# A rotation by 180 degrees: part of the first load moved to a second DMA queue

## The chip, the cores and the metric

The kernel runs on one core of a Trainium2 chip. The metric is device time in microseconds (us). "Span" is the profile's time from a core's first instruction to its last; it is about 1.8 us shorter than the device time of the same execution.

## The reference

```python
def setup_inputs():
    batch, c, h, w = 32, 3, 256, 256
    return {"x": np.random.randn(batch, c, h, w).astype(np.float32)}

def reference(x):
    return np.rot90(x, k=2, axes=(-2, -1)).astype(np.float32)
```

Each of the 96 planes of 256 x 256 elements, read as one row of 65,536 elements, has to come out reversed. That is 25.17 MB in and 25.17 MB out.

## The kernel before

The planes form three groups of 32. A group is a tile of 128 partitions by 16,384 elements (64 KB per partition), four partitions per plane. VectorE reverses each partition in place, swapping 2,048-element blocks through a scratch tile T; the store reverses the order of the four partitions of a plane.

```python
    A = pool.tile([P, E], x.dtype, tag="A")      # P = 128, E = 16384
    Bt = pool.tile([P, E], x.dtype, tag="B")
    Ct = pool.tile([P, E], x.dtype, tag="C")
    # ... T, back(), copy()
    def load(t, g, lo, hi):
        return nc.sync.dma_start(out=t[:, lo:hi], in_=x4[g][:, lo:hi])

    def store(t, g, lo, hi):
        return nc.sync.dma_start(
            out=o4[g][:, ::-1, lo:hi], in_=t[:, lo:hi])
    # ... inside(t): 12 copies on VectorE
    TAIL = 1536
    load(A, 0, 0, E)
    load(Bt, 1, 0, E)
    body = load(Ct, 2, 0, E - TAIL)
    load(Ct, 2, E - TAIL, E)
    inside(A)
    LEAD = 128
    store(A, 0, 0, LEAD)
    first = store(A, 0, LEAD, E)      # made to wait for `body`
    # ...
    for g, t in ((1, Bt), (2, Ct)):
        inside(t)
        store(t, g, 0, E)
```

All eight DMAs go through SyncE's queue. The big store of A waits until the body of C has landed; a last strip of C (6 KB per row) and a small store (512 B per row) are meant to keep the DMA engines busy while that store is issued.

Of the kernel before, what the change touches and what calls it, by code (L numbers as in the profile page):

```python
# [2 lines left out]

os.environ.setdefault("NEURON_RT_ULTRASERVER_MODE", "4")

# [4 lines left out]


@with_exitstack
def kernel(
    ctx: ExitStack,
    tc: tile.TileContext,
    x: bass.AP,
    out: bass.AP,
):








    nc = tc.nc
    P = 128

    B, C, H, W = x.shape
    L = H * W
    G = 32
    E = L // 4
    J = E // 8

    x4 = x.rearrange("b c h w -> (b c) (h w)").rearrange(
        "(g n) (s e) -> g (n s) e", n=G, s=4)
    o4 = out.rearrange("b c h w -> (b c) (h w)").rearrange(
        "(g n) (s e) -> g n s e", n=G, s=4)  # L40

    pool = ctx.enter_context(tc.tile_pool(name="slots", bufs=1))
    A = pool.tile([P, E], x.dtype, tag="A")
    Bt = pool.tile([P, E], x.dtype, tag="B")
    Ct = pool.tile([P, E], x.dtype, tag="C")
    T = pool.tile([P, J], x.dtype, tag="T")

    def back(t, lo, hi):
        return t[:, hi - 1:(lo - 1 if lo else None):-1]

    def copy(dst, src):
        tc.keep_in_program_order(nc.vector.tensor_copy(out=dst, in_=src))  # L52

    def load(t, g, lo, hi):
        return nc.sync.dma_start(out=t[:, lo:hi], in_=x4[g][:, lo:hi])  # L55

    def store(t, g, lo, hi):
        return nc.sync.dma_start(
            out=o4[g][:, ::-1, lo:hi], in_=t[:, lo:hi])

    def inside(t):
        for lo in range(0, E // 2, J):
            hi = E - lo - J
            copy(T[:, :], back(t, hi, hi + J))
            copy(t[:, hi:hi + J], back(t, lo, lo + J))
            copy(t[:, lo:lo + J], T[:, :])

    TAIL = 1536
    load(A, 0, 0, E)
    load(Bt, 1, 0, E)  # L70
    body = load(Ct, 2, 0, E - TAIL)
    load(Ct, 2, E - TAIL, E)
# [3 lines that stand above are left out]
    first = store(A, 0, LEAD, E)  # L76
    tc.add_manual_dep(
        first.ins, body.ins.name,
        mybir.DependencyInfo(mybir.DependencyClass.Sync, mybir.DependencyReason.DATA),
        reason="the first store is queued while the last strip is on its way")  # L80
# [5 lines that stand above are left out]
# [1 line left out]
_INS = ['x']  # L87
_OUTS = [((32, 3, 256, 256), 'float32')]


# [23 lines left out]
```

## Time and profile before

| | before |
|---|---|
| device time, median of 3 (lowest to highest) | 122.09 us (121.91 to 122.40) |
| span of the profiled execution | 120.2 us |
| VectorE busy | 44.2 us, 37% |
| DMA engines busy | 97.5% |
| first DMA packet, last completion write | 1.77 us, 119.05 us |

The last row comes from the trace's list of DMA packets: start, duration, size and queue of each. No view prints them, so they are given as numbers in the text. With each DMA, every one of the 16 DMA engines gets eight of the 128 rows, one packet per row, and ends it with a 4-byte completion write. The lines of the page itself are in the prediction.

### The profile page before, as it was taken

Reading aid. Unit: us, or ns where it says so; the run is one execution under the profiler, and the core shown is the slowest. Engines: PE = TensorE matmul, PEld = TensorE weight load, DVE = VectorE, ACT = ScalarE, POOL = GpSimd, SP = SyncE. Lnnn points to the kernel's source line nnn. Section 1 sums busy time; section 2 is a strip of 40 time slices with the busy share of each in tenths; the row PEclk is TensorE's granted clock in tenths of the full one; section 3 lists DMA queues with packets and bytes.
Section 4 is the critical chain, followed back from the end, with each engine's and each line's share of the span. In section 5 each row is a group of like instructions: output and inputs, shape, how many; then the busy total and the mean of one; then the engine's idle time right before and its main releaser. Section 6 shows DMA issues by size and latency. Waiting matters only on the chain.

```text
span 120.2 us, 95 instructions
## 1 busy us (share of the span) xinstructions
DVE 44.2 (37%) x36; POOL 0.2 (0%) x4
## 2 busy tenths in 40 slices
DVE  0000000499995099999059999400000000000000
POOL 0000000000000000000000000000000000000000
DMA  9889988898889879879499777988898889888980
GB/s 349 349 349 393 654 349 349 349 676 371 349 349 633 382 316 593 356 316 633 190 440 692 346 346 346 692 349 349 349 698 349 349 349 698 349 349 349 676 371 0
DMA packets 1152, 50.33 MB, mean 419 GB/s; under 512 B 128, under 2 KB 256, under 8 KB 384
## 3 DMA queue, kind: packets, MB, share of 16 engines
q1 hardware_dynamic: 1152, 50.33, 97.5%
HBM read 25.17 MB, written 25.17 MB: 419 GB/s over the span
## 4 chain that ended last, share of the span: by engine, by line
DMA 34%; DVE 25%; another core or an unknown queue 4%; issue 1%; SPq 0%; DVEq 0%
DMA Bt<-in_x_dram 34%; DVE T L52 8%; DVE Bt L52 8%; DVE Ct L52 8%; SPq L55 0%; DVEq L52 0%
## 5 line engine op out<-in xcount | busy, mean ns | idle before, releaser
L52 DVE COPY T<-A 128x2048 f32<-128x2048 f32 x4 | 4.9, 1227 | 22.7 <-DMA A<-in_x_dram 22.6
L52 DVE COPY T<-Ct 128x2048 f32<-128x2048 f32 x4 | 4.9, 1227 | 4.5 <-DMA Ct<-in_x_dram 4.4
L52 DVE COPY T<-Bt 128x2048 f32<-128x2048 f32 x4 | 4.9, 1227 | 4.4 <-DMA Bt<-in_x_dram 4.3
L52 DVE COPY Bt<-Bt 128x2048 f32<-128x2048 f32 x4 | 4.9, 1227 | 0.1
L52 DVE COPY A<-T 128x2048 f32<-128x2048 f32 x4 | 4.9, 1227 | 0.1
L52 DVE COPY Bt<-T 128x2048 f32<-128x2048 f32 x4 | 4.9, 1227 | 0.1
L52 DVE COPY Ct<-T 128x2048 f32<-128x2048 f32 x4 | 4.9, 1227 | 0.1
L52 DVE COPY Ct<-Ct 128x2048 f32<-128x2048 f32 x4 | 4.9, 1227 | 0.1
L52 DVE COPY A<-A 128x2048 f32<-128x2048 f32 x4 | 4.9, 1227 | 0.1
L98 POOL MEMSET const-bfloat16-1.0<- 128x1 bf16 x1 | 0.1, 102 | 0.0
L98 POOL MEMSET const-uint8-127<- 128x1 uint8 x1 | 0.1, 101 | 0.0
L98 POOL MEMSET const-float32-0.0<- 128x1 f32 x1 | 0.1, 99 | 0.2 <-issue 0.2
L98 POOL MEMSET const-float32-1.0<- 128x1 f32 x1 | 0.1, 98 | 0.0
## 6 DMA issues: line engine op xcount, KB each, us to landing
out_dram<-A SPq DMA_DIRECT2D x1, 8128.0 KB, 21.2
Ct<-in_x_dram SPq DMA_DIRECT2D x1, 7424.0 KB, 57.8
Ct<-in_x_dram SPq DMA_DIRECT2D x1, 768.0 KB, 59.3
out_dram<-A SPq DMA_DIRECT2D x1, 64.0 KB, 35.2
A<-in_x_dram SPq DMA_DIRECT2D x1, 21.9
Bt<-in_x_dram SPq DMA_DIRECT2D x1, 40.7
out_dram<-Bt SPq DMA_DIRECT2D x1, 39.9
out_dram<-Ct SPq DMA_DIRECT2D x1, 42.8
```

The lines of the kernel that those rows point to most:

```text
L52: tc.keep_in_program_order(nc.vector.tensor_copy(out=dst, in_=src))
L98: nc = _bacc.Bacc("TRN2", target_bir_lowering=False, num_devices=1)
```

## The change

The intent is to have two engines start the first load at the same time. ScalarE issues the first 2 KB of each row of A and SyncE the other 62 KB, so that the stream of data might begin sooner or denser.

```diff
-    def load(t, g, lo, hi):
-        return nc.sync.dma_start(out=t[:, lo:hi], in_=x4[g][:, lo:hi])
+    def load(t, g, lo, hi, queue=nc.sync):
+        return queue.dma_start(out=t[:, lo:hi], in_=x4[g][:, lo:hi])
@@
     TAIL = 1536
-    load(A, 0, 0, E)
+    HEAD = 512
+    load(A, 0, 0, HEAD, nc.scalar)
+    load(A, 0, HEAD, E)
     load(Bt, 1, 0, E)
```

## The prediction

> **What bounds the kernel now.** I read the page from the top: busy shares first, then the slices, the queue line, the chain, and last the trace's own list of DMA packets, which no view prints. Engines and data movement are told apart at once.
>
> ```profile
> span 120.2 us, 95 instructions
> DVE 44.2 (37%) x36; POOL 0.2 (0%) x4
> DMA  9889988898889879879499777988898889888980
> DMA packets 1152, 50.33 MB, mean 419 GB/s; under 512 B 128, under 2 KB 256, under 8 KB 384
> q1 hardware_dynamic: 1152, 50.33, 97.5%
> ```
>
> The reader is to see that VectorE works 37% of the span while the sixteen DMA engines are busy for 97.5% of it: 0.975 x 120.2 us = 117.2 us. The whole tensor goes in and out once (25.17 MB each way), so the bytes cannot shrink. There is one queue, q1: everything is issued by SyncE.
>
> The chain of waits in order of time begins like this (start, duration, what):
>
> ```profile
> 0.66 0.07 issue
> 0.73 0.39 SPq L55
> 1.12 0.06 issue
> 1.18 40.74 DMA Bt<-in_x_dram
> ```
>
> It then follows VectorE through groups B and C, which is only how the view walks back over semaphores. That VectorE does not set the end is seen from the last store: it is issued at 76.62 us, when the store of A, queued at 59.53, has not yet landed (59.53 plus 21.2 in the table of issues is 80.7), and B's lies behind that. The last store takes 42.8 us to land only because it queues. Cutting the span into stages shows the same; the columns are the stretch, its length, VectorE busy, GpSimd busy, clock, DMA share and GB/s:
>
> ```profile
> 0.00:1.20 1.20, 0.00 (x0) 0.20 (x4) 1.00 0.00 0
> 1.20:21.90 20.70, 0.00 (x0) 0.00 (x0) 1.00 0.99 415
> 21.90:59.50 37.60, 29.45 (x24) 0.00 (x0) 1.00 0.99 429
> 59.50:76.60 17.10, 14.72 (x12) 0.00 (x0) 1.00 1.06 456
> 76.60:119.40 42.80, 0.00 (x0) 0.00 (x0) 1.00 0.96 416
> 119.40:120.20 0.80, 0.00 (x0) 0.00 (x0) 1.00 0.00 0
> ```
>
> A packet is counted in whole, so shares over 1.00 are an artefact of where I cut. What matters: DMA is full from the first stage to the last, and bare only in the first one to two and the last one microsecond.
>
> From the packet records, counted from the span's start: the first packets start between 1.77 and 2.21 us (mean 1.93), and the last completion write ends at 119.05. The difference is 117.28 us, and each engine is on average busy for 117.17 us of it. So there is **no hole to fill between the first packet and the last**. The budget is 1.77 us of front, 117.28 us of packets, 1.14 us from the last packet to the end.
>
> One slow place stands inside the 117.28. A row of 64 KB is one packet; it takes 2.418 us from the second row on, but about 3.19 us for the first row of each engine, and the second row's packet starts on average 3.13 us after the first's (5.06 against 1.93). So the cold start of the stream costs 3.13 - 2.42 = 0.71 us, once. Only this and the front are anywhere near the changed load.
>
> The front is made of the barrier between engines, one DMA issue, and a latency. The timeline (start, duration, engine, line):
>
> ```profile
> 0.73 0.39 SPq L55 DMA_DIRECT2D A<-in_x_dram  x1
> 1.18 0.42 SPq L55 DMA_DIRECT2D Bt<-in_x_dram  x1
> 1.63 1.01 SPq L55 DMA_DIRECT2D Ct<-in_x_dram  x2
> ```
>
> SyncE starts its first issue at 0.73; the first packet starts 1.04 us later, at 1.77. The next issues are done at 2.64, long before the 20 us of A's packets run out, so issue time after the first never shows.
>
> **What the Trainium skill says.** The page "DMA: Bandwidth & Descriptors", section "Issuing engines are not separate DMA queues", says that DMAs started by different engines run on the same 16 DMA engines and that using several saves only sequencer time. The trace before has only one queue and cannot show it, but it shows how little sequencer time there is to save: one 0.39 us issue lies ahead of the first packet. The same page, section "Queues, rings and completion order", says each DMA engine alternates between the queues that have work, at packet granularity; no run here shows it yet. Section "Where 436 GB/s comes from" gives a ceiling of 435.2 GB/s for 16 ports. The trace agrees closely: 16 x 65,536 B / 2.418 us = 433.6 GB/s. Section "Latency and other measured facts" gives about 0.6 us to the first byte for DMAs from SyncE and ScalarE alike; here 0.65 us pass from the end of the first issue (1.12) to the first packet (1.77).
>
> **The change part by part.**
>
> *Added:* one DMA on ScalarE's queue, 128 rows of 2 KB. The order of instructions shows just that: one copy of 128x512 on ScalarE, SyncE's first copy now 128x15872 in place of 128x16384, everything else unchanged. In the trace before, ScalarE leaves the starting barrier at 0.652 us and SyncE at 0.647 (raw event times), so ScalarE should issue at about 0.74, beside SyncE and not ahead of it. Front saved: 0, because the head's first packet needs the same issue and the same latency.
>
> *Cost of the split:* each row becomes two packets. I fit the packet time from sizes in this trace: 512 B takes 27 ns, 6,144 B takes 234 ns, 65,536 B takes 2,418 ns. The line through the outer two is 8.2 ns + 36.8 ns per KB (6 KB: 229, close to 234). So a 2 KB packet takes about 82 ns, of which 8.2 is new. Eight rows per engine give 8 x 8.2 = 66 ns, plus one more completion write of 9 ns: **+0.07 us** of DMA time. This lies on the bounding path, as the stream has no slack.
>
> *Shape of the big load:* it is no longer contiguous in memory. The strided body of C was issued in 432 ns (raw), A in 387. If the first packet waits for the issue to end, SyncE's part begins 45 ns later, but the head is then already in work. I take +0.02 us.
>
> *Cold start:* 0.71 us are lost on each engine's first packet. If that is latency of the first read, both queues pay it at once and nothing changes. If it is a ramp with too few reads in flight, two queues with one packet each could shorten it. I give this an expected **-0.15 us**, from a fifth of 0.71; this is my choice, not a measurement.
>
> *VectorE:* its first copy waits for the end of A at 22.6 us and would move by about 0.1. It waits again at 42.0 and 61.5 for loads, so the shift is absorbed. C's last copy ends at 76.6, while the store of A lands only at 80.7 and B's at 100, so there is over 20 us of slack. The store's waiting for the body of C at 59.5 shifts along with the stream.
>
> The sum is 0 + 0.07 + 0.02 - 0.15 = -0.06 us on 122.09, rounded to **122.0 us**.
>
> **The rivals.**
>
> *The head fills the front.* If SyncE's 64 KB issue were slow because of its size, 2 KB rows could start flowing sooner. For it: 1.04 us from issue to packet is long. Against it: SyncE's four load issues take 387 to 533 ns, and the shortest rows (6 KB) took the longest, so rows' length is not what an issue costs. It would be worth 0.2 to 0.4 us, so some 121.7 to 121.9.
>
> *The second queue gets in the way.* Both issuing engines make descriptors at the same moment; if that is shared work, each engine's first packets come later. The first packets of one DMA already spread over 0.44 us, so a second could add about as much. Switching between queues after each packet may also break read-ahead: with 16 switches of, say, 20 to 50 ns, 0.3 to 0.8 us would be lost. The trace of one queue does show packets back to back, so it has something to lose. This makes 122.4 to 122.9.
>
> *ScalarE issues late.* Then its packets mix into the stream later, and A lands by the same total of bytes. The time stays at 122.1 to 122.2, as no hole opens.
>
> **Range and chances.** The executions of the kernel before spread from 121.91 to 122.40, so the noise alone is about 0.25 either way. The first rival pulls down by 0.3, the second up by 0.5. I take 121.6 to 122.5. To be 2% faster, 2.4 us would have to go; the whole front and the cold start together are 1.77 + 0.71 = 2.48 us, most of it barrier and latency that the change doesn't touch. To be 2% slower, the head would have to cost 2.4 us, about 30 times its worked-out cost of packets. So: faster 0.01, same 0.98, slower 0.01.
>
> **What would show each step right or wrong.** A second queue should appear with 128 packets and 0.26 MB. The first packet should start within 0.1 us of 1.77; clearly earlier, by 0.2 or more, means the first rival. Busy time of the DMA engines should grow by under 0.1 us each; if it grows by 0.3 or more, switching queues costs. The second row of 62 KB should start later than the first by as much as before, less 2 KB's worth; a shorter distance means that the cold start is a ramp. VectorE's first copy should begin within 0.3 us of 22.6 and the last store be issued near 76.6. The prediction fails if the stream gets a hole of microseconds anywhere, most likely around 20 to 22 us, where A hands over to B, or if ScalarE's queue needs some setting-up that SyncE's doesn't.

## The result, and the profile after

| | before | after |
|---|---|---|
| device time, median of 6 (lowest to highest) | 122.12 us (121.91 to 122.65) | 122.01 us (121.96 to 122.07) |
| ratio, 95% interval | | 0.9983 (0.9963 to 1.0003) |
| first packet, last completion write | 1.77 us, 119.05 us | 1.76 us, 119.06 us |
| DMA busy per engine | 117.17 us | 117.24 us |

A ratio is taken from the runs of both kernels in the same rounds, so it is not quite the ratio of the medians quoted.

The page of the changed kernel, the lines that answer to those of before:

```profile
span 120.2 us, 97 instructions
DVE 44.2 (37%) x36; POOL 0.2 (0%) x4
DMA  9888988899889879979499777988898889888990
DMA packets 1296, 50.33 MB, mean 419 GB/s; under 512 B 144, under 2 KB 272, under 8 KB 528
q1 hardware_dynamic: 1152, 50.07, 97.0%
q10 hardware_dynamic: 144, 0.26, 0.6%
```

A second queue, q10, has appeared with 128 packets of 2 KB and 16 completion writes. The shares add up to 97.6%, where one queue had 97.5%: the same work, spread over two queues. The timeline of the start (start, duration, engine, line):

```profile
0.73 0.38 ACTq L55 DMA_DIRECT2D A<-in_x_dram  x1
0.73 0.39 SPq L55 DMA_DIRECT2D A<-in_x_dram  x1
1.18 0.42 SPq L55 DMA_DIRECT2D Bt<-in_x_dram  x1
...
22.62 1.23 DVE L52 COPY T<-A 128x2048 f32<-128x2048 f32 x1 [22.62 <-DMA A<-in_x_dram]
```

Both issues start at 0.73 us. SyncE issues no earlier and no faster than before, and VectorE gets A at 22.62 us in both kernels. The same stages as before (stretch, length, VectorE, GpSimd, clock, DMA share, GB/s):

```profile
0.00:1.20 1.20, 0.00 (x0) 0.20 (x4) 1.00 0.00 0
1.20:21.90 20.70, 0.00 (x0) 0.00 (x0) 1.00 1.01 423
21.90:59.50 37.60, 29.45 (x24) 0.00 (x0) 1.00 0.98 423
59.50:76.60 17.10, 14.67 (x12) 0.00 (x0) 1.00 1.07 459
76.60:119.40 42.80, 0.05 (x1) 0.00 (x0) 1.00 0.96 416
119.40:120.20 0.80, 0.00 (x0) 0.00 (x0) 1.00 0.00 0
```

No stage got shorter. The first seems denser (1.01 against 0.99) and the second thinner by the same, because whole packets fall to one side of the cut. The issues of A with their KB and the time to landing:

```profile
A<-in_x_dram SPq DMA_DIRECT2D x1, 7936.0 KB, 21.9
...
A<-in_x_dram ACTq DMA_DIRECT2D x1, 256.0 KB, 22.0
```

This pair says most: 256 KB took as long to land as 7,936 KB. The packet list shows why. Each engine begins with a 62 KB packet of SyncE's queue, then takes one 2 KB packet of ScalarE's, then again one of SyncE's, and so on for eight rows. The "head" is not ahead: its first packet starts at 4.78 us, when the first 62 KB packet ends, and its last one ends with A.

In the kernel before, the two lines to compare with, of its issues and of its timeline, are:

```profile
A<-in_x_dram SPq DMA_DIRECT2D x1, 21.9
...
22.62 1.23 DVE L52 COPY T<-A 128x2048 f32<-128x2048 f32 x1 [22.62 <-DMA A<-in_x_dram]
```

### The profile page after: what moved, and what is told of

Same layout as the page of the kernel before. It is cut to its first block, busy times and chain, and to the rows that moved or that the text cites. A ratio compares the mean times of both kernels' runs of the same rounds, so it can differ in the third digit from the quotient of the medians.

```text
span 120.2 us, 97 instructions
## 1 busy us (share of the span) xinstructions
DVE 44.2 (37%) x36; POOL 0.2 (0%) x4
## 4 chain that ended last, share of the span: by engine, by line
DMA 34%; DVE 25%; another core or an unknown queue 4%; issue 1%; SPq 0%; DVEq 0%
DMA Bt<-in_x_dram 34%; DVE T L52 8%; DVE Bt L52 8%; DVE Ct L52 8%; SPq L55 0%; DVEq L52 0%
```

## The experiments

My theory: the DMA stream bounds the kernel from its first packet to its last; front and cold start are the same for one queue and two; the split costs a few nanoseconds per packet. Rival one: the second queue fills the front or shortens the cold start, and the split hides part of the gain. Rival two: turns between queues cost time, and some gain at the start hides that.

### The split alone, on one queue

```diff
-    load(A, 0, 0, HEAD, nc.scalar)
+    load(A, 0, 0, HEAD)
     load(A, 0, HEAD, E)
```

> The same split (2 KB and 62 KB per row), but both loads from SyncE's queue, head first. Theory (the stream bounds, a packet costs 8.2 ns more, front and cold start are common to both queues): 122.1 to 122.2 us, mean DMA busy per engine 117.24 us as in the changed kernel, ratio to the kernel before 0.998 to 1.002. First row of packets: the 2 KB packet absorbs the cold start and takes about 0.7 + 0.08 us. Rival (the second queue fills the front or shortens the cold start): this kernel loses what the second queue gained, so 0.1 to 0.4 us slower than the changed kernel of the same rounds, and the first megabyte lands later.

Measured: 122.12 us (121.96 to 122.64), before 122.17, ratio 0.9994 (0.9973 to 1.0015). Against the kernel before, moving the split back to one queue changes nothing that these rounds resolve, and against the changed kernel of the same rounds (122.10) it loses nothing: the 0.1 to 0.4 us of rival one is not seen. The other sign named for rival one did appear: the first megabyte (10^6 bytes) was in at 5.52 us, against 5.14 to 5.23 in three traces of the changed kernel. That mark is coarse, because packets count when they end, and here eight heads per engine end before any 62 KB packet does. My detail missed: the sixteen 2 KB packets that start first took 0.08 to 0.51 us (mean 0.19), not 0.78. Yet A was landed, on average over the engines, at 21.92 us, as in the three kernels with unsplit rows (21.92 to 21.96). So the cold start isn't a fixed delay charged to whichever packet is first; it is spread over the packets of the first microseconds.

### The changed kernel again, and the kernel before as its own rival

No edit: the changed kernel and the kernel before are each run as an experiment.

> The changed kernel itself in more rounds, beside the kernel before. Theory: the 0.11 us by which its median was lower is noise, the true difference is +0.07 us from the split; ratio 0.998 to 1.002 with 1 inside the interval. Rival (a real gain from the second queue): ratio about 0.998 again, with 1 outside the interval.

> The kernel before, unchanged, submitted as if it were an experiment: shows how far two equal kernels differ in the same rounds. Every theory expects 1.000; the deviation seen is the noise that a difference of 0.1 us has to be held against. I expect up to 0.2%.

Measured: changed kernel 122.10 us, ratio 0.9990 (0.9971 to 1.0009); kernel before against itself 122.11 us, ratio 0.9987 (0.9969 to 1.0004). In these rounds a kernel "beats" its own copy by 0.13%. A single ratio of 0.998 proves nothing here.

### The roles swapped

```diff
-    load(A, 0, 0, HEAD, nc.scalar)
-    load(A, 0, HEAD, E)
+    load(A, 0, 0, HEAD)
+    load(A, 0, HEAD, E, nc.scalar)
```

> The 2 KB heads from SyncE's queue and the 62 KB parts from ScalarE's, while the loads of B and C follow on SyncE's. Theory: the two queues alternate packet by packet, eight packets each, so A still lands at 22 us, and the time is 122.1 to 122.2 us, busy 117.24 us per engine. Which packet comes first tells whether SyncE's queue always goes first (then 2 KB first) or ScalarE's, or the larger. Rival (second queue gets in the way of the first): the queue with B's packets behind it takes turns beyond the heads, A lands late (up to 40 us), and the time may grow by some tenths.

Measured: 122.50 us (121.94 to 122.62), ratio 1.0013 (0.9992 to 1.0034): unresolved, at most a third of a percent slower. My detail missed again. The timeline of this kernel, VectorE's first copy:

```profile
25.66 1.23 DVE L52 COPY T<-A 128x2048 f32<-128x2048 f32 x1 [25.66 <-DMA A<-in_x_dram]
```

A was usable 3 us later than in the changed kernel. In the packet list, the sixteen packets that start first are again of SyncE's queue, as in the changed kernel, so it is the queue and not the size that went first in these two. The engines took 32 heads, two each on average, before their first 62 KB packets, so the heads ran out one row early. The last 62 KB packets of A start at 19.76 us on average, but the completion write that reports them comes at 24.52: one 64 KB packet of B, 2.4 us long, goes between. Five of six runs were 122.34 or slower, so I suspect a real loss of a few tenths. In the profiled execution the engines' completions of A were spread over 1.22 us, against 0.44 in the changed kernel; why this matters is taken up below.

### Many turns between queues, and the same pieces on one queue

```diff
-    load(A, 0, 0, HEAD, nc.scalar)
-    load(A, 0, HEAD, E)
+    CHUNK = 512
+    for odd, queue in ((1, nc.scalar), (0, nc.sync)):   # one queue: nc.sync twice
+        pieces = A[:, :].rearrange("p (k two c) -> p k two c", two=2, c=CHUNK)
+        source = x4[0].rearrange("p (k two c) -> p k two c", two=2, c=CHUNK)
+        queue.dma_start(out=pieces[:, :, odd, :], in_=source[:, :, odd, :])
```

> A is loaded in 2 KB pieces, odd pieces from ScalarE's queue, even ones from SyncE's: 256 packets per engine for A in place of 8. Theory: 248 more packets of 8.2 ns each give +2.03 us, so 124.1 us, busy 119.2 us per engine. Rival (changing between queues costs 20 to 50 ns a time): up to 255 changes cost 5 to 13 us more, 129 to 137 us, and the difference to the same pieces on one queue shows it alone.

> The same 2 KB pieces of A, odd and even ones as two loads, both from SyncE's queue. Theory: 124.1 us as with two queues, equal within 0.2 us. Rival (changing queues costs): faster than with two queues by 5 us or more. If several pieces are put into one packet, the packet count stays well under 256 per engine and the cost is less than 2.03 us.

Measured: two queues 124.51 us, ratio 1.0190 (1.0176 to 1.0204); one queue 124.59 us, ratio 1.0195 (1.0181 to 1.0209). The queue lines, first of two queues, then of one:

```profile
q1 hardware_dynamic: 3072, 46.14, 88.3%
q10 hardware_dynamic: 2064, 4.19, 9.5%
```

```profile
q1 hardware_dynamic: 5136, 50.33, 97.9%
```

The packets number 3072 + 2064 = 5136 in both. ScalarE's queue ran alone at first, this time: 349 of its packets, some 22 per engine, start before SyncE's first one at 4.64 us. From 8 to 20 us, wherever the packet list shows without doubt which packet follows on the same engine, it is one of the other queue (141 of 141). So about 210 turns per engine were made, and they cost nothing: 0.08 us less than one queue, where rival two asked for 5 us or more. That settles the price of a turn for 2 KB packets. The price of packets is confirmed and sized: A was landed, mean over engines, 22.13 us after the mean of the sixteen earliest packet starts in place of 20.04, which is 2.09 us for 248 more packets, or 8.4 ns each. Busy time per engine missed: 120.21 us with two queues and 120.27 with one, where 119.2 was expected. A 2 KB packet here took 88 ns (median) against 84 in the changed kernel. The expected 124.1 us fell short by 0.4, because these DMAs also begin later. The timeline of the kernel with two queues:

```profile
0.73 0.66 SPq L73 DMA_DIRECT2D A<-in_x_dram  x1
0.73 0.61 ACTq L73 DMA_DIRECT2D A<-in_x_dram  x1
1.45 11.58 SPq L55 DMA_DIRECT2D Bt<-in_x_dram  x1
```

An issue of 16 pieces per row takes 0.61 to 0.66 us in place of 0.39, and the first packet starts at 2.14 us in place of 1.77. So the front was longer with the longer issue, as the prediction's first rival thought, but cutting rows lengthens it. The issues account for 0.22 to 0.27 us of the 0.37; the rest is not explained.

### Half of A from each queue

```diff
-    HEAD = 512
+    HEAD = 8192
```

> HEAD of 32 KB in place of 2 KB: half of each row of A from each queue. Theory: the number of packets is what costs, so again +0.07 us, 122.1 to 122.2 us, busy 117.24 us, A lands at 22 us. Rival (the second queue helps by the bytes it has in flight at the start): the cold start shortens, first megabyte by 4.9 us or sooner in place of 5.2 to 5.3, time down by 0.1 to 0.4 us.

Measured: 121.98 us (121.92 to 122.09), before 122.21, ratio 0.9983 (0.9970 to 0.9995). The interval just leaves 1 out, which by itself speaks for rival one. But the first megabyte was in at 5.18 us, and at 5.14 to 5.23 us in the three traces of the changed kernel, against 5.32 to 5.40 in three traces of unsplit rows on one queue. As said, that mark is coarse. A's landing, mean over engines, is at 21.97 us, not earlier than the 21.92 to 21.96 of those one-queue kernels. Where the 0.1 us arises is taken up below.

### ScalarE alone

```diff
-        return nc.sync.dma_start(...)      # load and store
+        return nc.scalar.dma_start(...)
```

> The kernel before with every load and store issued by ScalarE in place of SyncE: one queue, unsplit rows. Theory: front and cold start belong to the path and not to SyncE, so the first packet starts at 1.75 to 1.85 us and the time is 122.0 to 122.3 us. Rival (ScalarE's queue has setting-up or latency of its own, hidden in the changed kernel because SyncE's packets came first): first packet at 2.0 us or later and the time longer by as much.

Measured: 122.20 us, before 122.21, ratio 0.9999 (0.9986 to 1.0011); first packet at 1.75 us. ScalarE's queue is as good as SyncE's and has no setting-up of its own. The front belongs to the path.

### A beside B

```diff
-    load(A, 0, 0, E)
+    load(A, 0, 0, E, nc.scalar)      # whole rows; B and C stay on SyncE's queue
```

> The kernel before with only A's load moved to ScalarE's queue, whole rows, while SyncE loads B and C: A's and B's packets should alternate. Theory: A lands at about 41 us in place of 22, VectorE starts 19 us later, its copies run from 41.5 to 87 us without a pause; but B's store is ready at 72 us (needed at 80) and C's at 87 us (needed at 100), so the time stays 122.0 to 122.2 us: the slack of VectorE that the prediction used. Rival (VectorE's start matters, an early first group is worth something): longer by a microsecond or more.

Measured: 122.05 us (121.90 to 122.12), before 122.20, ratio 0.9987 (0.9974 to 0.9999). The timeline of this kernel:

```profile
42.17 1.23 DVE L52 COPY T<-A 128x2048 f32<-128x2048 f32 x1 [42.17 <-DMA A<-in_x_dram]
...
45.94 14.18 SPq L58 DMA_DIRECT2D out_dram<-A  x2
...
87.56 0.54 SPq L58 DMA_DIRECT2D out_dram<-Ct  x1
```

VectorE starts 19.6 us later than in the kernel before, the last store is issued 10.9 us later (87.56 against 76.62), and the time isn't longer. This is the strongest evidence on the change's intent: getting the first group sooner can't pay while the stream is full, as getting it 19.6 us later costs nothing.

### The scatter, and a wider strip

What is left is about 0.1 us between kernels with one queue and with two. I took from the packet lists the landing of A (mean of the engines), the end of C's body on its slowest engine, and the start of the last completion write (0.01 us before its end), in us:

| kernel | queues for loads | A landed | C's body, slowest | last completion | difference of the last two |
|---|---|---|---|---|---|
| before | 1 | 21.96 | 59.09 | 119.04 | 59.95 |
| before again | 1 | 21.92 | 59.41 | 119.38 | 59.97 |
| all on ScalarE | 1 | 21.92 | 59.18 | 119.16 | 59.98 |
| split on SyncE | 1 | 21.92 | 59.26 | 119.28 | 60.02 |
| after | 2 | 21.98 | 59.20 | 119.05 | 59.85 |
| after again | 2 | 21.95 | 58.99 | 118.92 | 59.93 |
| after, third | 2 | 21.99 | 59.35 | 119.20 | 59.85 |
| half and half | 2 | 21.97 | 59.13 | 119.01 | 59.88 |
| A beside B | 2 | 41.27 | 59.17 | 119.11 | 59.94 |
| swapped | 2 | 24.52 | 59.68 | 119.59 | 59.91 |

The columns are read as follows. The end follows the slowest engine's body of C: the difference stays within 0.17 us, while the ends differ by up to 0.67. That fits the program, since A's big store is issued only once the body has landed on every engine. The spread of the engines is mostly set in the first packets and is carried along (after: 0.44 us at A, 0.57 at C's body; swapped: 1.22 and 1.19). Idle time between 59.5 and 62 us (fewer than 16 packets under way, averaged over the 16 engines) was 0.00 and 0.10 us in two traces of the kernel before, 0.01, 0.01 and 0.05 in three of the changed kernel's, and 0.40 in the swapped one; the expectation below counted it slightly higher. A wider strip of C should give the store time to be queued, and remove this:

```diff
-    TAIL = 1536
+    TAIL = 3072
```

> The kernel before with the last strip of C 12 KB wide in place of 6 KB. In the traces so far the engines stood idle for 0.01 to 0.42 us on average around 60 us, between the last load packets and the first packets of A's store, because that store is issued only when the slowest engine has landed C's body; the end of the run moves with it. Theory of the scatter: with 16 rather than 8 packets' worth of strip the store is queued in time, the idle time there is under 0.02 us, and the time is 121.8 to 122.0 us with less scatter than the kernel before. Rival (the scatter of some tenths comes from elsewhere, such as the HBM or the ends of the run): no change in median or scatter.

> The changed kernel with the same 12 KB strip. Theory: what little the second queue seemed to give (about 0.1 us, seen with 2 KB and 32 KB heads) is only the luck of that hand-over at 60 us, so with the hand-over mended both kernels are equal within 0.1 us, this one 0.02 to 0.07 us slower for its 8 more packets per engine. Rival (the second queue gives a real 0.1 us at the start): this one is 0.1 us faster than the kernel before with the same strip.

> The changed kernel once more, for a third set of rounds beside the kernel before. Theory: 122.0 to 122.2 us, ratio 0.998 to 1.001; slower than both kernels with the wider strip by 0.1 to 0.2 us.

Measured: kernel before with the wider strip 123.04 us (122.69 to 123.36), ratio 1.0072 (1.0055 to 1.0090); changed kernel with it 122.55 us (122.34 to 123.14), ratio 1.0044 (1.0021 to 1.0067); changed kernel itself 121.99 us, ratio 0.9986 (0.9974 to 0.9998), with 1 just outside the interval as in two other runs with two queues. My theory of a cure fell: both became slower. The idle time did go (0.00 us in each), but something worse came. Packets of the strip took 0.50 us on average where the median is 0.46, and one engine fell behind the rest: in the profiled execution of the first kernel it finished at 119.85 us, the other fifteen by 119.33. The windows around the hand-over, first of the kernel before, then with the wider strip:

```profile
57.00:59.00 2.00, 0.12 (x1) 0.00 (x0) 1.00 0.16 61
59.00:60.00 1.00, 0.00 (x0) 0.00 (x0) 1.00 1.02 412
60.00:61.00 1.00, 0.00 (x0) 0.00 (x0) 1.00 2.48 1028
```

```profile
57.00:59.00 2.00, 0.22 (x1) 0.00 (x0) 1.00 1.01 393
59.00:60.00 1.00, 0.00 (x0) 0.00 (x0) 1.00 1.05 381
60.00:61.00 1.00, 0.00 (x0) 0.00 (x0) 1.00 0.93 382
```

From 59 to 60 us, with the store now issued (at 57.8 us) and the strip still loading, the engines are as full as before but carry 381 GB/s in place of 412. The 0.16 and 2.48 before are again whole packets counted by where they start. The slow packets follow the early store in time, but that it slows them isn't shown, and one trace speaks against it: in the kernel before, twelve strip packets took 0.26 to 0.37 us in place of 0.23, and ten of them start before the big store is issued at 59.53 us. The cause stays open. Between the two wider-strip kernels the one with two queues is 0.5 us faster, against my expectation of equality; with ranges that overlap and the cause of the slow packets open, I don't read more into it. The strip of 6 KB stays, and no version here beats both kernels clearly.

## Why the prediction was right

**The bound.** Right. The stream of packets runs from 1.76 to 119.06 us in the changed kernel as in the one before, and neither VectorE 19.6 us later (A beside B, 119.11 us) nor another issuing engine (all on ScalarE, 119.16) moved the end out of the scatter (before again, 119.38).

**The front, 0 us saved.** Right. Both engines issue at 0.73 us, and the first packet is at 1.76 us.

**The shape of the big load, +0.02 us.** This small term was wrong. SyncE's issue of A took 387 ns in both kernels, so nothing was delayed. Nor would a head "already in work" have covered a delay: in the changed kernel no head starts before 4.78 us.

**The cost of the split, +0.07 us.** Right in kind, too large in size for this case. Busy time per engine grew by 0.065 us from the first trace to the second, but that it agrees is luck: it is 117.17 and 117.32 us in two traces of the kernel before, and 117.24, 117.15 and 117.30 in three of the changed one. It also counts the overlap of packets twice. The interval from one row to the next (mean over engines, rows 2 to 8) is 2,415.0 ns before and 2,418.8 ns after, the same to 0.3 ns in three traces of unsplit rows and three of the changed kernel: 3.8 ns per row, **0.03 us** for eight rows. In the run of many small packets the 8.2 ns was about right (8.4). The fit has a slip of units, which does not touch the 8.2: 36.8 ns is per 1,000 bytes and was multiplied by KB of 1,024. Put right, the line gives 234 ns for 6 KB, just as measured, and 84 for 2 KB, which is what the new packets took.

**The cold start, -0.15 us.** This term was wrong. From the mean first packet to the mean start of the second big packet it took 3.13, 3.14 and 3.09 us with unsplit rows and 3.11, 3.10 and 3.08 us in three traces of the changed kernel. The gain is 0.02 us, within the scatter. Even that hangs on single engines whose first packet starts late (at 2.82 us in the changed kernel), which moves the mean start: the second big packets start at 5.06, 5.01 and 5.01 us with unsplit rows and at 5.04, 5.01 and 5.05 in the changed kernel. Of the two readings that the prediction left open, "a ramp that two queues shorten" did not come about: on every engine of the changed kernel the second queue's first packet starts only when the first big one ends (4.78 us at the earliest), so there were never two at work to shorten it; "latency of the first read" isn't shown either, since with 2 KB packets in front on one queue the loss was spread over several packets.

**VectorE's slack, over 20 us.** Right as far as it was tried: in A beside B the last store is issued 10.9 us later and costs nothing. The full 20 us were not tried.

**The rivals.** A turn between queues costs nothing that can be measured. The head did not fill the front; in the changed kernel it never came first. ScalarE did not issue late (0.73 us, as SyncE), yet its packets mixed into the stream as that rival described, and the time stayed.

**The sum.** -0.06 us was predicted and -0.11 measured (medians), so 122.0 came out to the tenth, though not by the terms given: that agreement is luck, and what the prediction had right is that nothing on the bounding path changes by more than about 0.1 us. Over all the rounds, 17 runs of the changed kernel average 122.04 us and 44 of the kernel before (six of them the copy of it) 122.19. The other two-queue kernels, half and half and A beside B, average 122.02 and the other one-queue kernels, split on SyncE and all on ScalarE, 122.19, with 11 runs each. So there may be some 0.15 us, 0.12%, in a second queue. Against it stands the swapped kernel, which has two queues too and averages 122.42, and the 0.13% by which the kernel before "beat" itself. If it is real, the table places it after 58 us and not at the start: A lands no earlier, and C's slowest body ends on average 0.07 us earlier (59.17 against 59.24, five traces without the swapped one against four), which is within the scatter. The rest of the run is 0.09 us shorter (59.85 to 59.94 against 59.95 to 60.02, without overlap). From the first engine's last completion write to the last engine's it takes 0.18 to 0.34 us with two queues and 0.31 to 0.41 with one. Why the engines end more evenly when the load of A used a second queue stays open, as does whether a handful of profiled executions represents the rest.

## What to carry to other kernels

Where DMA engines are busy from the first packet to the last, as here, a second queue for the first load has nothing to fill: look for time ahead of the first packet that it could shorten and for holes between packets, and if there are none, expect next to nothing (here about 0.1%, if it is real). Size the cost of cutting a transfer from the interval between packets (3.8 ns per row here), not from their durations (8.2 ns), because those overlap. When a small ratio is in question, run the kernel before against itself first; here that alone gave 0.9987.

## What the Trainium skill lacked or had wrong

- "DMA: Bandwidth & Descriptors", "Queues, rings and completion order": it has an engine drain "a whole packet (≈9-17 descriptors typical, spec ceiling ≤64)" from one queue before it turns to the next. Alternation at packet granularity is confirmed, but each packet in the changed kernel's records is a single row of a DMA, 62 KB or 2 KB, and the turn comes after every one; how many descriptors such a packet holds, the trace doesn't say. The page doesn't say which of two queues begins, nor for how long it runs alone when both issues start together: in the swapped kernel two 2 KB packets per engine, on average, went ahead of the first 62 KB packet and A was usable 3 us later, and with many small packets ScalarE's queue ran alone until 4.64 us. Whether the other queue's packets were ready by then, no run shows.
- Same section: it gives no cost of a turn. The runs show none: 124.51 us with 2 KB packets on two queues, 124.59 on one.
- "DMA: Bandwidth & Descriptors", "Latency and other measured facts": its 0.6 us to the first byte agrees (0.65 us after the end of the first issue), but it doesn't say from where it counts (from the start of the issue it is 1.04 us), nor has it the cold start behind that, about 0.7 us per engine, nor that the issue itself grows with the pieces per row (0.39 us for one, 0.61 to 0.66 for 16).
- "Perfetto Trace Analysis", "DMA Instruction — HWDGE (DVE, Sync)", has a descriptor buffer that can be full while an issue is still being made, but no page that I read gives a figure for how long that can hold an issue up: after 2,048 packets of A on SyncE's queue and as many on ScalarE's, SyncE's issue of B took 11.58 us in place of 0.42. That a full buffer is the cause isn't shown.
- No page that I read has the slow packets at the end of the loads: strip packets of 12 KB took 0.50 us on average where the median is 0.46, and the cause is open.
